# One decoder block in float32 on one core: the work at its stage boundaries put in an explicit order

## The chip, the cores and the metric

The kernel runs on one core of one Trainium2 chip. The metric is the device time of one launch in microseconds (us). The engines are TensorE (PE, with its weight loads as PEld), VectorE (DVE), ScalarE (ACT), GpSimd (POOL) and SyncE (SP, which here only issues DMAs). Each engine takes its own instructions in program order; between engines there are semaphores.

## The reference

One decoder block for 256 tokens, width 2048, all in float32. Cut to what matters:

```python
u = rmsnorm(h, g_mix_pre)
qa, ka, va, qb, kb, vb, ga, gb = split(u @ w_in)          # 2048 x 10240
oa = moba_attention(rope(qa), rope(ka), va)               # one block of 256: causal softmax
ob = diff_attention(rope(qb), rope(kb), vb, lam, diff_subln_g)
mixed = sigmoid(ga) * (oa @ w_br_moba) + sigmoid(gb) * (ob @ w_br_diff)
h = h + rmsnorm(mixed @ w_out, g_mix_post)
u2 = rmsnorm(h, g_mlp_pre)
h = h + rmsnorm(square(relu(u2 @ w_up)) @ w_down, g_mlp_post)      # 2048 x 8192 and back
gate = sigmoid(rmsnorm(h, g_ple_pre) @ w_ple_gate)
h = h + rmsnorm((p @ w_ple_proj) * gate, g_ple_post)
```

## The kernel before

**Products.** PE multiplies float32 numbers split in two: `hi` is the value rounded to PE's short format (a copy by ACT, line 211 for weights), `lo` is the rest (a subtraction by DVE, line 214). A product takes three matmuls per 128 rows of weights: hi by hi, hi by lo, lo by hi (lines 259 to 261). The 256 tokens are two halves, m = 0 and m = 1. A weight matrix is cut in chunks of 512 columns, a chunk in sub-blocks of 256 rows (512 KB, two 128-row pieces). One sub-block and one half make six matmuls of 512 columns.

**Weights.** `convert` (line 199) issues the DMA of one sub-block on SP into one of 5 `raw` buffers, then ACT's copy and DVE's subtraction into one of 8 `whi`/`wlo` pairs. `ensure` (line 217) calls it for sub-blocks up to a given distance ahead of the one that PE takes. In the first chunk one 128-row piece of the `lo` of sub-blocks 2 to 7 goes to POOL (`c.pool`).

**Activations.** `turn` (line 177) transposes 512 columns of one half with four PE transposes into one PSUM bank (tag `aux`, 4 banks in rotation). `turned` (line 183) empties it. With a gain vector (the norm's weight, one value per partition after the transpose) that is three instructions: DVE multiplies the bank by the gain into `ug` in SBUF (line 188), ACT copies `ug` to `hi` (line 173), DVE subtracts for `lo` (line 174). This happens for x at the start (8 such blocks), for h between the attention part and the MLP (8), and for h between the MLP and the last gate (8). The norm's 1/rms factor is applied later, to the product.

**Start.** PE runs some warm-up matmuls on zeros, x's first 128 x 512 block is loaded and turned, then the first chunk of w_in begins. The hook `first` (line 556) places the other transposes and `turned` calls in the first chunk: the two blocks of group kg before the step of sub-block 2 kg - 1.

**Stage boundaries.** The last chunk of w_out (`o_ch[3]`) and the last of w_down (`dn_ch[3][3]`) finish half 0 before half 1. `post` of a half sums squares (ACT, line 661), multiplies by the gain (DVE, line 722 or 812), and starts `residual` (line 670): a reduction and eleven small DVE instructions for the 1/rms (`rstd`, line 138), four additions of 512 columns (line 677), then transposes and `turned`. `residual` is a generator that `tick` moves on after steps of the matmul loop, so its instructions land between those of two small products (`pp_ch`, four steps of six matmuls) and of the next chunk (`up_ch[0]` or `pg_ch[0]`), whose first six sub-blocks are done for half 0 first, then for half 1 (`lead=6`). `rms_h` then sums the squares of the new h.

**End.** The last chunk of the gate (`pg_ch[3]`) also finishes half 0 first; each half then has a sigmoid, a product, a sum of squares, the 1/rms chain, four additions and four output DMAs on SP (line 863).

**Order.** Everything is in program order. The tile library adds the waits: an instruction waits for what it reads, and for whoever used the buffer before.

Of the kernel before, what the change touches and what calls it, by code (L numbers as in the profile page):

```python
# [31 lines left out]
KT = 2  # L32
# [8 lines left out]
WAIT = (3, 7)  # L41
# [23 lines left out]
class Chunk:  # L65


    def __init__(self, w, kts, col, src, lead=0, trail=0):
        self.w, self.kts, self.col, self.src = w, kts, col, src
        self.post = self.hook = self.ahead = None  # L70
        self.pool = {}
# [9 lines left out]
def tile_hybrid_block(ctx: ExitStack, tc: tile.TileContext, a, out: bass.AP):  # L81
# [28 lines left out]
    nc.sync.dma_start(gr[0], a["g_mix_pre"][0].rearrange("(k p) -> k p", p=P))  # L110
# [85 lines left out]
    state = {"conv": 0, "used": 0}  # L196
    tasks = deque()

    def convert(i):
        c, s = todo[i]  # L200
        kts = c.subs[s]
        n = len(kts)
        raw = wp.tile([P, KT, CW], F32, name="raw", tag="raw", bufs=NRAW)
        k0 = kts[0] * P
        nc.sync.dma_start(raw[:, :n, :], c.w[k0:k0 + n * P, c.col:c.col + CW].rearrange("(k p) c -> p k c", p=P))
        hi = wp.tile([P, KT, CW], F32R, name="whi", tag="whi", bufs=NB)
        lo = wp.tile([P, KT, CW], F32R, name="wlo", tag="wlo", bufs=NB)
        np_ = c.pool.get(s, 0)
        cuts = [slice(j, j + 1) for j in range(n)] if i < 2 else [slice(0, n)]
        for j in cuts:  # L210
            act.activation(hi[:, j], raw[:, j], AF.Copy)  # L211
        for j in cuts if np_ in (0, n) else [slice(0, np_), slice(np_, n)]:
            eng = nc.gpsimd if j.start < np_ else dve
            eng.tensor_sub(lo[:, j], raw[:, j], hi[:, j].bitcast(F32))  # L214
        conv[i] = (hi, lo)

    def ensure(i):
        last = min(i, state["used"] + NB - 1, len(todo) - 1)
        while state["conv"] <= last:
            convert(state["conv"])  # L220
            state["conv"] += 1

# [20 lines left out]
    def run(c):  # L243
# [4 lines left out]
        for s, m in c.order:  # L248
            i = c.base + s
            if c.hook:  # L250
                c.hook(s, m)
            ensure(i + (c.ahead(s, m) if c.ahead else AHEAD))
            hi, lo = conv[i]
            for j, kt in enumerate(c.subs[s]):
                ah, al = c.src.get(kt, m)
                first = done[m] == 0
                done[m] += 1
                last = done[m] == len(c.kts)
                pe.matmul(acc[m], lhsT=ah, rhs=hi[:, j, :], start=first, stop=False)  # L259
# [272 lines left out]
    pg_ch = [Chunk(w_pg, all_kt, n * CW, None, lead=6 if n == 0 else 0, trail=6 if n == 3 else 0) for n in range(4)]  # L532
# [8 lines left out]
    for c in (up_ch[0], pg_ch[0]):  # L541
        c.ahead = lambda s, m: 3 if m == 0 and s < 5 else AHEAD
# [113 lines left out]
    def newstat(name):  # L656
        return [sm.tile([P, 4], F32, name=f"{name}{m}", tag=f"{name}{m}", bufs=1) for m in range(2)]

    def sq_acc(src, dst):
        j = sm.tile([P, CW], F32, name="sq", tag="w2", bufs=4)  # L660
        act.activation(j, src, AF.Square, accum_out=dst)

    def total_rstd(ss, m, name):
        t = sm.tile([P, 1], F32, name="tot", tag="tot", bufs=2)
        dve.tensor_reduce(t, ss[m], AX.X, ALU.add)
        r = sm.tile([P, 1], F32, name=name, tag=f"{name}{m}", bufs=1)
        rstd(t, D, r, "n")
        return r

    def residual(m, og, ss, dst, gain, name):  # L670

        r = total_rstd(ss, m, name)
        t_ps = {}

        def add(kg):
            s = slice(kg * CW, (kg + 1) * CW)
            dve.scalar_tensor_tensor(h[m][:, s], og[m][:, s], r, h[m][:, s], op0=ALU.mult, op1=ALU.add)  # L677

        if m == 0:
            for kg in range(4):  # L680
                add(kg)
        for i in range(WAIT[m]):
            yield
            if m and i in (1, 2, 3, 4):
                add(i - 1)
        for i in range(5):
            if i:
                turned(t_ps.pop(i - 1), dst, i - 1, m, gain)
            if i < 4:
                t_ps[i] = turn(h[m][:, i * CW:(i + 1) * CW])  # L690
            yield
# [21 lines left out]
    resid = {}  # L713
    ss_o = newstat("sso")

    def post_out(n):
        gb = bcast("g_mix_post", n)

        def post(m, acc):
# [10 lines left out]
    o_ch[0].hook = settle  # L730
    for n, c in enumerate(o_ch):
# [67 lines left out]
    def post_dn(g, n):  # L799
        gb = bcast("g_mlp_post", n) if g == 3 else None  # L800

        def post(m, acc):
# [7 lines left out]
            if g == 3:  # L810
                sq_acc(og[m][:, s], ss_f[m][:, n:n + 1])
                dve.tensor_mul(og[m][:, s], og[m][:, s], gb)
                if n == 3:
                    resid[m] = start(residual(m, og, ss_f, u3T, 2, "r3"))
                    if m:
                        pg_ch[0].hook = settle_rms(start(rms_h(rs3, "rs3")))
        return post

    def settle_rms(t):
        def hook(s, m):  # L820
            if (s, m) == (7, 0):
                finish(t)
        return hook
# [22 lines left out]
    ss_e = newstat("sse")  # L846

    def post_pg(n):
        gb = bcast("g_ple_post", n)

        def post(m, acc):
            s = slice(n * CW, (n + 1) * CW)
            e = E[n][:, m, :]
            act.activation(og[m][:, s], acc, AF.Sigmoid, scale=rs3[m])
            dve.tensor_mul(e, e, og[m][:, s])
            sq_acc(e, ss_e[m][:, n:n + 1])
            dve.tensor_mul(og[m][:, s], e, gb)
            if n == 3:
                r = total_rstd(ss_e, m, "re")
                for kg in range(4):  # L860
                    s = slice(kg * CW, (kg + 1) * CW)
                    dve.scalar_tensor_tensor(og[m][:, s], og[m][:, s], r, h[m][:, s], op0=ALU.mult, op1=ALU.add)
                    nc.sync.dma_start(out[0, m * P:(m + 1) * P, s], og[m][:, s])
        return post

    for n, c in enumerate(pg_ch):
        c.src, c.post = u3T, post_pg(n)
        run(c)
# [25 lines left out]
```

## Time and profile before

| what | value |
| --- | --- |
| time, median of 3 runs | 1509.63 us (1509.37 to 1509.73) |
| the profiled execution's own time | 1509.84 us |
| its span, first to last instruction | 1508.1 us |
| PE busy | 1480.8 us, 98% |
| DVE busy | 864.5 us, 57% |
| ACT busy | 698.2 us, 46% |
| POOL busy | 10.8 us, 1% |
| mean DMA rate | 187 GB/s |
| mean granted TensorE clock | 0.995 |

A PE row's duration is that of one matmul through the array; matmuls overlap, so the distance from one start to the next is what one costs. For ACT and DVE a row's duration is a little longer than the distance between two rows that follow each other.

### The profile page before, as it was taken

What the parts mean: (1) busy time and instruction counts of PE and PEld (TensorE: products, weight loads), DVE (VectorE), ACT (ScalarE), POOL (GpSimd) and SP (SyncE); (2) the same over time, 40 slices, a digit from 0 to 9 for tenths busy, and PEclk for the clock granted to TensorE, in tenths of its full rate; (3) what the DMA queues carried; (4) which work ended last, traced back from release to release, by engine and by line L of the source; (5) the groups of instructions that cost most, each with busy time, mean ns of one, the idle gap of its engine ahead of it and who ended that gap; (6) DMA issues with size and microseconds to landing.
All of it is one profiled execution on the core that took longest, in us unless ns stands there. A gap on an engine that the chain in (4) does not pass through costs nothing.

```text
span 1508.1 us, 18344 instructions
## 1 busy us (share of the span) xinstructions
PE 1480.8 (98%) x7065; PEld 1237.2 (82%) x7065; DVE 864.5 (57%) x1074; ACT 698.2 (46%) x920; POOL 10.8 (1%) x10
## 2 busy tenths in 40 slices
PE   8999999999999999998999999999999999999897
PEld 6888888888888888877888888888888888887785
DVE  5764646565444665567564456554655555655774
ACT  5654545444544344436444445433544344543552
POOL 2000000000000000000000000000000000000000
PEclk9999999999999999999999999999999999999998
DMA  7855555555565656735566555656456646566372
GB/s 255 264 160 179 166 181 162 178 174 178 167 217 181 200 182 240 235 113 181 183 217 196 186 184 182 205 185 199 165 181 221 195 148 218 180 208 205 101 235 77
DMA packets 146087, 282.11 MB, mean 187 GB/s; under 512 B 8864, under 2 KB 10064, under 8 KB 145744
## 3 DMA queue, kind: packets, MB, share of 16 engines
q1 hardware_dynamic: 146000, 280.95, 57.8%
q8 instruction: 55, 0.90, 0.3%
q14 instruction: 32, 0.26, 0.1%
HBM read 278.81 MB, written 2.10 MB: 186 GB/s over the span
## 4 chain that ended last, share of the span: by engine, by line
PE 92%; DVE 4%; issue 1%; ACT 1%; POOL 0%; DMA 0%; POOLq 0%; SPq 0%; DVEq 0%; ACTq 0%
PE acc L260 22%; PE acc L261 22%; PE acc L259 22%; PE acct L285 15%; PE acct L286 7%; PE s_ps L360 1%; DVE wlo L214 1%; DVE h L677 1%; PE t_ps L180 1%; DVE ug L188 1%; ACT u L173 1%; POOL wlo L214 0%; PE qk_ps L328 0%; DVE u L174 0%; ACT whi L211 0%
## 5 line engine op out<-in xcount | busy, mean ns | idle before, releaser
L214 DVE TENSOR_TENSOR wlo<-raw,whi 128x1024 fp32r<-128x1024 f32 (+1 forms) x518 | 615.3, 1214 | 426.8 <-ACT whi L211 426.2
L211 ACT ACTIVATE whi<-raw 128x1024 fp32r<-128x1024 f32 (+1 forms) x518 | 531.0, 1051 | 403.8 <-PE acc L261 280.6
L285 PE MATMUL acct<-u,whi 128*128 128x512 f32 x960 | 339.6, 399 | 0.6 <-ACT r L767 0.6
L259 PE MATMUL acc<-whi,u 128*128 128x512 f32 x800 | 319.5, 399 | 5.4 <-ACT whi L211 5.4
L260 PE MATMUL acc<-wlo,u 128*128 128x512 f32 x800 | 313.5, 392 | 3.8 <-DVE wlo L214 2.2
L261 PE MATMUL acc<-whi,u 128*128 128x512 f32 x800 | 313.6, 392 | 0.0
L286 PE MATMUL acct<-u,wlo 128*128 128x256 f32 x960 | 269.6, 281 | 0.0
L285 PEld LDWEIGHTS acct<-u,whi 128*128 128x128 f32 x960 | 180.4, 188 | 45.8 <-ACT r L767 0.9
L259 PE MATMUL acc<-whi,h 128*128 128x512 f32 x512 | 199.2, 389 | 0.0
L260 PE MATMUL acc<-wlo,h 128*128 128x512 f32 x512 | 199.2, 389 | 0.0
L261 PE MATMUL acc<-whi,h 128*128 128x512 f32 x512 | 199.2, 389 | 0.0
L286 PEld LDWEIGHTS acct<-u,wlo 128*128 128x128 f32 x960 | 181.3, 189 | 0.2
L259 PEld LDWEIGHTS acc<-whi,u 128*128 128x128 f32 x800 | 151.0, 189 | 36.1 <-ACT whi L211 5.8
L260 PEld LDWEIGHTS acc<-wlo,u 128*128 128x128 f32 x800 | 151.2, 189 | 35.3 <-DVE wlo L214 3.0
L261 PEld LDWEIGHTS acc<-whi,u 128*128 128x128 f32 x800 | 151.0, 189 | 32.6 <-DVE u L174 0.8
L261 PEld LDWEIGHTS acc<-whi,h 128*128 128x128 f32 x512 | 96.1, 188 | 20.1
L259 PEld LDWEIGHTS acc<-whi,h 128*128 128x128 f32 x512 | 96.1, 188 | 20.1
L260 PEld LDWEIGHTS acc<-wlo,h 128*128 128x128 f32 x512 | 96.1, 188 | 19.8
L784 ACT ACTIVATE r<-acct 128x256 f32<-128x256 f32 x60 | 22.8, 380 | 69.2 <-PE acct L286 69.2
L785 DVE TENSOR_TENSOR r<-acct,r 128x256 f32<-128x256 f32 x60 | 24.7, 423 | 51.1 <-ACT r L784 51.1
L259 PE MATMUL acc<-whi,o 128*128 128x512 f32 x128 | 50.4, 394 | 0.0
L259 PE MATMUL acc<-whi,m 128*128 128x512 f32 x128 | 50.1, 391 | 0.0
(153 smaller groups left out, 921.6 us busy)
## 6 DMA issues: line engine op xcount, KB each, us to landing
raw<-in_w_in SPq DMA_DIRECT2D x160, 512.0 KB, 4.3
raw<-in_w_up SPq DMA_DIRECT2D x128, 512.0 KB, 4.2
raw<-in_w_down SPq DMA_DIRECT2D x128, 512.0 KB, 5.1
raw<-in_w_out SPq DMA_DIRECT2D x32, 512.0 KB, 5.3
raw<-in_w_ple_gate SPq DMA_DIRECT2D x32, 512.0 KB, 5.6
raw<-in_w_br_moba SPq DMA_DIRECT2D x16, 512.0 KB, 4.5
raw<-in_w_br_diff SPq DMA_DIRECT2D x16, 512.0 KB, 4.8
h<-in_x SPq DMA_DIRECT2D x2, 1024.0 KB, 10.2
```

Source lines behind the costliest of these rows:

```text
L173: act.activation(hi, src, AF.Copy)
L180: pe.transpose(t_ps[:, j * P:(j + 1) * P], src[:, j * P:(j + 1) * P], ident)
L188: dve.tensor_mul(ug, t_ps, gT[gain][:, 4 * kg:4 * kg + 4].unsqueeze(2).to_broadcast([P, 4, P]))
L211: act.activation(hi[:, j], raw[:, j], AF.Copy)
L214: eng.tensor_sub(lo[:, j], raw[:, j], hi[:, j].bitcast(F32))
L259: pe.matmul(acc[m], lhsT=ah, rhs=hi[:, j, :], start=first, stop=False)
L260: pe.matmul(acc[m], lhsT=ah, rhs=lo[:, j, :], start=False, stop=False)
L261: pe.matmul(acc[m], lhsT=al, rhs=hi[:, j, :], start=False, stop=last)
L285: pe.matmul(acc[q].rearrange("p a t -> p (a t)"), lhsT=hi[:, j, ws], rhs=mv, start=first, stop=False)
L286: pe.matmul(acc[q][:, 0], lhsT=lo[:, j, ws], rhs=mv[:, 0:T], start=False, stop=last)
L784: act.activation(r[:, q % 2], acc[:, 1], AF.Copy)
L785: dve.tensor_add(r[:, q % 2], acc[:, 0], r[:, q % 2])
```

## The change

Five things change. (1) `turned` with a gain no longer has a DVE multiplication: for each of the four 128 x 128 transposes in the bank, ACT copies with the gain as its scale straight from PSUM to `hi`, and DVE computes bank times gain minus `hi` straight from PSUM to `lo`, in the order ACT, DVE, ACT, DVE and so on. (2) `rstd` has eight small instructions instead of eleven, and the reduction over the chunks goes ahead of the last chunk (`rests`). (3) At both boundaries a class `Boundary` with a written-out script replaces `residual` and `tick`; `convert` is cut into `head` (DMA if not yet issued, and ACT's copies) and `low` (DVE's subtractions), which the script places apart. In the script T is `turn`, U is `turned`, A is one addition, each with (half, column group); H(s) and L(s) are `head` and `low` of sub-block s of the next chunk. `run` calls a step's entries after its matmuls and its `post`; `before` runs `rests` at step (2, 0), and `done(m)` runs the 1/rms chain and, for half 0, its four additions. (4) At the start the first x block and the first weight sub-block are loaded in halves, two DMAs go to ACT's queue, and POOL's share of the `lo` work goes to DVE. (5) The last chunk does half 1 in two column halves of 256, and the sum of squares of the first of them is folded in early; two of the last five output DMAs are issued by ACT.

```diff
-    def rstd(ss, n, out_ap, tag):
+    def rstd(ss, n, out_ap, tag, rest=None):
         w = ss.shape[-1]
         v = sm.tile([P, w], F32, name="v", tag=f"v{tag}", bufs=2)
-        dve.tensor_scalar(v, ss, 1.0 / n, EPS, op0=ALU.mult, op1=ALU.add)
-        yi = sm.tile([P, w], I32, name="yi", tag=f"yi{tag}", bufs=2)
-        dve.tensor_scalar(yi, v.bitcast(I32), 1, None, op0=ALU.logical_shift_right)
+        dve.tensor_scalar(v, ss, -0.5 / n, -0.5 * EPS if rest is None else rest, op0=ALU.mult, op1=ALU.add)
         y = sm.tile([P, w], F32, name="y", tag=f"y{tag}", bufs=2)
-        dve.tensor_scalar(y.bitcast(I32), yi, -1.0, 1597463007.0, op0=ALU.mult, op1=ALU.add)
-        dve.tensor_scalar(v, v, -0.5, None, op0=ALU.mult)
+        dve.tensor_scalar(y.bitcast(I32), v.bitcast(I32), -0.5, 519526879.0, op0=ALU.mult, op1=ALU.add)
...
-    def turned(t_ps, dst, kg, m, gain=None):
+    def turned(t_ps, dst, kg, m, gain=None, js=range(4)):
         s = slice(m * P, (m + 1) * P)
-        if gain is not None:
-            ug = sm.tile([P, 4, P], F32, name="ug", tag="w2", bufs=4)
-            dve.tensor_mul(ug, t_ps, gT[gain][:, 4 * kg:4 * kg + 4].unsqueeze(2).to_broadcast([P, 4, P]))
-            t_ps = ug
-        split(dst.hi[kg][:, :, s], dst.lo[kg][:, :, s], t_ps)
+        if gain is None:
+            split(dst.hi[kg][:, :, s], dst.lo[kg][:, :, s], t_ps)
+            return
+        for j in js:
+            g = gT[gain][:, 4 * kg + j:4 * kg + j + 1]
+            hi = dst.hi[kg][:, j, s]
+            act.activation(hi, t_ps[:, j], AF.Copy, scale=g)
+            dve.scalar_tensor_tensor(dst.lo[kg][:, j, s], t_ps[:, j], g, hi.bitcast(F32), op0=ALU.mult, op1=ALU.subtract)
...
+    def head(i):
...
+        for j in cuts:
+            act.activation(hi[:, j], raw[:, j], AF.Copy)
+        conv[i] = (hi, lo, raw, cuts)
+    def low(i):
+        hi, lo, raw, cuts = conv[i]
+        for j in cuts:
+            dve.tensor_sub(lo[:, j], raw[:, j], hi[:, j].bitcast(F32))
...
     for c in (up_ch[0], pg_ch[0]):
-        c.ahead = lambda s, m: 3 if m == 0 and s < 5 else AHEAD
+        c.ahead = lambda s, m: 0 if m == 0 and s < 6 else AHEAD
...
     def first(s, m):
+        if (s, m) == (0, 1):
+            xt[1] = turn(x_sb[0][:, 0, 1])
+            turned(xt[1], uT, 0, 1, 0)
...
-    load_x0(0)
-    warm(4)
+    for j in range(2):
+        nc.sync.dma_start(x_sb[0][:, 0, 0, j * 256:(j + 1) * 256], x_d[0:P, j * 256:(j + 1) * 256])
+        load(0, j)
+    nc.scalar.dma_start(x_sb[0][:, 0, 1], x_d[P:T, 0:CW])
+    loads(2)
+    load_x(1)
+    warm(8)
     setup_gain(0)
-    t_ps = [turn(x_sb[0][:, 0, 0])]
-    turned(t_ps[0], uT, 0, 0, 0)
-    ensure(0)
-    load_x0(1)
-    warm(3)
-    t_ps.append(turn(x_sb[0][:, 0, 1]))
-    turned(t_ps[1], uT, 0, 1, 0)
-    ensure(1)
-    load_x(1)
+    warm(2)
+    xt[0] = turn(x_sb[0][:, 0, 0])
+    head(0)
+    turned(xt[0], uT, 0, 0, 0, range(2))
+    low(0)
+    turned(xt[0], uT, 0, 0, 0, range(2, 4))
-    c_in[0].ahead = lambda s, m: (2, 2, 2, 2, 2, 2, 4, 5)[s]
-    c_in[0].pool = {i: 1 for i in range(2, 8)}
+    c_in[0].ahead = lambda s, m: (2 * m, 2, 2, 2, 2, 2, 4, 5)[s]
...
+    class Boundary:
+        def __init__(self, last, pps, nxt, ss, dst, gain, name):
+            A, T, U = self.add, self.turn, self.turned
+            H, L = (lambda s: lambda: hd(nxt, s)), (lambda s: lambda: lw(nxt, s))
+            last.hook = self.before     
+            last.script = {(7, 1): [H(3)]}
+            pps[0].script = {(0, 0): [T(0, 0)], (0, 1): [T(0, 1), U(0, 0), H(4), U(0, 1)]}
+            pps[1].script = {(0, 0): [T(0, 2), L(3), A(1, 0), A(1, 1), U(0, 2)],
+                             (0, 1): [T(0, 3), H(5), L(4), A(1, 2), A(1, 3), U(0, 3), L(5)]}
+            nxt.script = {(0, 0): [T(1, 0)], (1, 0): [T(1, 1), U(1, 0)], (2, 0): [T(1, 2), U(1, 1)],
+                          (3, 0): [T(1, 3), U(1, 2)], (4, 0): [U(1, 3)]}
...
-                resid[m] = start(residual(m, og, ss_o, u2T, 1, "r2"))
-                if m:
-                    start(rms_h(rs2, "rs2"))
+                bd.done(m)
...
+                if (g, n) == (0, 1):
+                    start(rms_h(rs2, "rs2"))
...
+    def run_last(c):
+        acc = [ps.tile([P, CW], F32, name="acc0", tag="acc", bufs=4)]
+        acc += [ps.tile([P, CW // 2], F32, name=f"acc1{k}", tag="acc", bufs=4) for k in range(2)]
+        parts = [(0, 0, CW), (1, 0, CW // 2), (1, CW // 2, CW)]
+        order = [(s, q) for s in range(2) for q in range(3)] + [(s, q) for q in range(3) for s in range(2, n)]
...
+                for i, (a, b) in enumerate(((0, 512), (512, 1024), (1024, 1536), (1536, 1792), (1792, 2048))):
+                    s = slice(a, b)
                     dve.scalar_tensor_tensor(og[m][:, s], og[m][:, s], r, h[m][:, s], op0=ALU.mult, op1=ALU.add)
-                    nc.sync.dma_start(out[0, m * P:(m + 1) * P, s], og[m][:, s])
+                    (nc.scalar if m and i % 2 else nc.sync).dma_start(out[0, m * P:(m + 1) * P, s], og[m][:, s])
```

## Rows read from the trace of the kernel before

**Rows 1.** Busy time by stretch; columns: stretch, its length, each engine's busy time (count).

```profile
9.06:37.45 28.39, 26.80 (x123) 21.02 (x121) 18.61 (x27) 17.78 (x30) 10.58 (x6) 1.00 0.81 268
660.70:701.57 40.87, 37.11 (x172) 30.02 (x170) 30.06 (x56) 20.83 (x40) 0.00 (x0) 0.96 0.30 93
1388.19:1431.50 43.31, 37.78 (x171) 29.93 (x170) 31.63 (x58) 20.84 (x41) 0.00 (x0) 0.96 0.30 100
```

**Rows 2.** Waits of PE from 660 to 706 us: total, times, longest.

```profile
PE acc L259 <- ACT whi L211: 2.2, 1, 2.2
PE acc L260 <- DVE wlo L214: 1.1, 1, 1.1
PE acct L285 <- ACT r L767: 0.6, 1, 0.6
```

**Rows 3.** Timeline of PE, spacing of matmuls (start, duration) at both clock levels.

```profile
682.25 0.63 PE L259 MATMUL acc<-whi,u 128*128 128x512 f32 x1
682.67 0.63 PE L260 MATMUL acc<-wlo,u 128*128 128x512 f32 x1
...
701.34 0.39 PE L261 MATMUL acc<-whi,u 128*128 128x512 f32 x1
701.57 0.39 PE L285 MATMUL acct<-u,whi 128*128 128x512 f32 x1
...
701.91 0.40 PE L285 MATMUL acct<-u,whi 128*128 128x512 f32 x1
```

**Rows 4.** Waits of DVE from 590 to 664 us.

```profile
DVE og L722 <- ACT sq L661: 12.0, 7, 2.5
```

**Rows 5.** Instruction groups by form: busy, mean ns; then idle before them.

```profile
L371 ACT ACTIVATE S<-S,nb 128x256 f32<-128x256 f32 x16 | 8.0, 502 | 17.5 <-DVE nb L368 17.5
L371 ACT ACTIVATE S<-S,nb 128x128 f32<-128x128 f32 x16 | 6.3, 393 | 11.4 <-DVE nb L368 11.4
L784 ACT ACTIVATE r<-acct 128x256 f32<-128x256 f32 x60 | 22.8, 380 | 69.2 <-PE acct L286 69.2
L211 ACT ACTIVATE whi<-raw 128x1024 fp32r<-128x1024 f32 x514 | 528.8, 1054 | 403.8 <-PE acc L261 280.6 <-PE acct L285 66.8 <-DMA raw<-in_w_down 32.0
...
L785 DVE TENSOR_TENSOR r<-acct,r 128x256 f32<-128x256 f32 x60 | 24.7, 423 | 51.1 <-ACT r L784 51.1
L445 DVE SCALAR_TENSOR_TENSOR ob<-o_ps,rd,gsub 128x256 f32<-128x256 f32 x8 | 3.3, 477 | 0.1
L318 DVE TENSOR_TENSOR t<-st,con 128x128 f32<-128x128 f32 x8 | 2.3, 285 | 0.0
L214 DVE TENSOR_TENSOR wlo<-raw,whi 128x1024 fp32r<-128x1024 f32 x508 | 607.7, 1223 | 423.5 <-ACT whi L211 423.1
```

**Rows 6.** DMA issues of the page: queue, count, KB each, median us to landing.

```profile
raw<-in_w_in SPq DMA_DIRECT2D x160, 512.0 KB, 4.3
```

**Rows 7.** Timeline of the start.

```profile
8.06 1.13 ACT L211 ACTIVATE whi<-raw 128x512 fp32r<-128x512 f32 x2
...
14.04 0.68 DVE L188 TENSOR_TENSOR ug<-t_ps,gT 128x512 f32<-128x512 f32 x1
14.75 0.63 ACT L173 ACTIVATE u<-ug 128x512 fp32r<-128x512 f32 x1 [1.36 <-DVE ug L188]
...
16.03 0.69 DVE L188 TENSOR_TENSOR ug<-t_ps,gT 128x512 f32<-128x512 f32 x1
```

**Rows 8.** Timeline of DVE at the first boundary.

```profile
662.23 0.14 DVE L665 TENSOR_REDUCE tot<-sso 128x1 f32<-128x4 f32 x1
...
663.03 0.27 DVE L151 TENSOR_SCALAR t<-v,y 128x1 f32<-128x1 f32 x1
...
664.54 2.74 DVE L677 SCALAR_TENSOR_TENSOR h<-og,r,h 128x512 f32<-128x512 f32 x4
```

**Rows 9.** Timeline of the end: ACT, then SP's output DMAs.

```profile
1497.15 0.69 ACT L854 ACTIVATE og<-acc,rs 128x512 f32<-128x512 f32 x1 [5.99 <-PE acc L261]
...
1503.13 1.66 SPq L863 DMA_DIRECT2D out<-og  x3
```

More of the change, by code (lines that the diff above doesn't have):

```diff
@@ L40 @@
 TRAIL = 3
-WAIT = (3, 7)
 C_ID = 0
@@ L70, in __init__ @@
         self.post = self.hook = self.ahead = None
-        self.pool = {}
+        self.script = {}
         self.fine = len(kts) == 2
@@ L219, in ensure, with hd, lw @@
         while state["conv"] <= last:
-            convert(state["conv"])
+            heads(state["conv"])
+            low(state["conv"])
             state["conv"] += 1
+    def hd(c, s):
+        assert c.base + s < state["used"] + NB and state["head"] == c.base + s
+        heads(c.base + s)
+    def lw(c, s):
+        assert state["conv"] == c.base + s
+        ensure(c.base + s)
     def tick():
@@ L269, in run @@
                 tick()
+            for f in c.script.get((s, m), ()):
+                f()
     def run_t(c):
@@ L666, in total_rstd, with rests @@
+    def rests(ss, k):
+        out = []
+        for m in range(2):
+            t = sm.tile([P, 1], F32, name="tot", tag=f"tot{m}", bufs=1)
+            dve.tensor_reduce(t, ss[m][:, 0:k], AX.X, ALU.add)
+            dve.tensor_scalar(t, t, -0.5 / D, -0.5 * EPS, op0=ALU.mult, op1=ALU.add)
+            out.append(t)
+        return out
+    def total_rstd(ss, m, rest, name):
         r = sm.tile([P, 1], F32, name=name, tag=f"{name}{m}", bufs=1)
-        rstd(t, D, r, "n")
+        rstd(ss, D, r, "n", rest[m])
@@ L668, in total_rstd, with before, done, add @@
         return r
[L670 to L691, printed above, removed]
+    class Boundary:
+        def __init__(self, last, pps, nxt, ss, dst, gain, name):
+            self.r, self.t_ps, self.ss, self.dst, self.gain, self.name = {}, {}, ss, dst, gain, name
+            A, T, U = self.add, self.turn, self.turned
[7 more added lines that the diff above has]
+                          (3, 0): [T(1, 3), U(1, 2)], (4, 0): [U(1, 3)]}
+        def before(self, s, m):
+            if (s, m) == (2, 0):
+                self.rest = rests(self.ss, 3)
+        def done(self, m):
+            self.r[m] = total_rstd(self.ss[m][:, 3:4], m, self.rest, self.name)
+            if m == 0:
+                for kg in range(4):
+                    self.add(0, kg)()
+        def add(self, m, kg):
+            def f():
+                s = slice(kg * CW, (kg + 1) * CW)
+                dve.scalar_tensor_tensor(h[m][:, s], og[m][:, s], self.r[m], h[m][:, s], op0=ALU.mult, op1=ALU.add)
+            return f
+        def turn(self, m, kg):
+            def f():
+                self.t_ps[m, kg] = turn(h[m][:, kg * CW:(kg + 1) * CW])
+            return f
+        def turned(self, m, kg):
+            return lambda: turned(self.t_ps.pop((m, kg)), self.dst, kg, m, self.gain)
@@ L813, in post, with norm3 @@
                 if n == 3:
-                    resid[m] = start(residual(m, og, ss_f, u3T, 2, "r3"))
-                    if m:
-                        pg_ch[0].hook = settle_rms(start(rms_h(rs3, "rs3")))
-        return post
[L819 to L823, printed above, removed]
+                    bd.done(m)
+        return post
+    def norm3():
+        t = start(rms_h(rs3, "rs3"))
+        pg_ch[0].hook = lambda s, m: finish(t) if (s, m) == (7, 0) else None
     u3T = None
@@ L846, in tile_hybrid_block, with before_last, post_pg, post @@
     ss_e = newstat("sse")
-    def post_pg(n):
-        gb = bcast("g_ple_post", n)
-        def post(m, acc):
-            s = slice(n * CW, (n + 1) * CW)
-            e = E[n][:, m, :]
+    rest_e = []
+    def before_last(s, m):
+        if (s, m) == (2, 0):
+            rest_e.extend(rests(ss_e, 3))
+    def post_pg(n, halves):
+        gb = bcast("g_ple_post", n)
+        def post(m, acc, k=0):
+            w = acc.shape[-1]
+            c = slice(k * w, (k + 1) * w)
+            s = slice(n * CW + k * w, n * CW + (k + 1) * w)
+            e = E[n][:, m, c]
@@ L862, in post @@
                     dve.scalar_tensor_tensor(og[m][:, s], og[m][:, s], r, h[m][:, s], op0=ALU.mult, op1=ALU.add)
-                    nc.sync.dma_start(out[0, m * P:(m + 1) * P, s], og[m][:, s])
+                    (nc.scalar if m and i % 2 else nc.sync).dma_start(out[0, m * P:(m + 1) * P, s], og[m][:, s])
         return post
-    for n, c in enumerate(pg_ch):
-        c.src, c.post = u3T, post_pg(n)
-        run(c)
+    def run_last(c):
+        n = len(c.subs)
+        acc = [ps.tile([P, CW], F32, name="acc0", tag="acc", bufs=4)]
+        acc += [ps.tile([P, CW // 2], F32, name=f"acc1{k}", tag="acc", bufs=4) for k in range(2)]
+        parts = [(0, 0, CW), (1, 0, CW // 2), (1, CW // 2, CW)]
+        order = [(s, q) for s in range(2) for q in range(3)] + [(s, q) for q in range(3) for s in range(2, n)]
+        for s, q in order:
+            m, c0, c1 = parts[q]
+            c.hook(s, q)
+            ensure(c.base + n - 1)
+            hi, lo = conv[c.base + s]
+            for j, kt in enumerate(c.subs[s]):
+                ah, al = c.src.get(kt, m)
+                pe.matmul(acc[q], lhsT=ah, rhs=hi[:, j, c0:c1], start=kt == 0, stop=False)
+                pe.matmul(acc[q], lhsT=ah, rhs=lo[:, j, c0:c1], start=False, stop=False)
+                pe.matmul(acc[q], lhsT=al, rhs=hi[:, j, c0:c1], start=False, stop=kt == NT - 1)
+            if q == 2:
+                del conv[c.base + s]
+                state["used"] = c.base + s + 1
+            if s == n - 1:
+                c.post(m, acc[q], max(q - 1, 0))
@@ L869, in tile_hybrid_block @@
+    for n, c in enumerate(pg_ch):
+        c.src, c.post = u3T, post_pg(n, n == 3)
+        if n < 3:
+            run(c)
+    c.hook = before_last
+    run_last(c)
     while tasks:
```

65 lines of the change are left out of this document (37 added, 28 removed).

## The prediction

> **What bounds the kernel now.** I read the stretches of the span first, then what PE waits for in the short ones, then the timelines of ACT and DVE there. From 37.45 to 660.70 us and from 705.1 to 1388 us PE has next to no gap, and one 512-column matmul costs 0.227 us (start to start) [rows 3]; nothing that the change does there can be seen. What can move are four places: the start (first product at 9.06 us, first chunk done at 37.45, 1.6 us of gaps between [rows 1]), the two stage boundaries, and the end. A boundary holds 138 matmuls of 0.227 and eight groups of four transposes, each group 0.45 us dearer than none: 34.9 us. The first lasts 40.87 us, the second 43.31 [rows 1], so 5.9 and 8.4 us are lost there. [...]
>
> **The new `turned`, the term that decides.** Before, one block of 4 x 128 columns is DVE 0.68, ACT 0.63, DVE 0.69 us, each starting 0.03 to 0.04 after the one before; the next block follows after 1.99 us [rows 7]. After, it is four ACT and four DVE pieces, all reading one PSUM bank. The question is whether ACT's piece j+1 may run beside DVE's piece j. The trace has one like case: `og` (DVE) and `sq` (ACT) both only read `acc`, no data pass between them, and still DVE waits for the end of `sq`, 7 times out of 8 [rows 4]. So two engines that read one bank are put in program order. I take it to hold for DVE then ACT, and for different columns of a bank, neither of which a row shows. Then the eight pieces are one chain.
>
> A piece of ACT: a 128-column row with a per-partition operand takes 0.393 from SBUF; a 256-column copy from PSUM without one takes 0.380, less 128 columns at 0.109 (502 - 393) is 0.27 [rows 5]. Bounds 0.27 and 0.39; I take 0.36, near the row that has the pointer. A piece of DVE: 0.285 without a pointer, and 0.477 at 256 columns with one, less 0.138 (423 - 285), is 0.34 [rows 5]; I take that, lower bound 0.285. With two hand-overs of 0.04 a pair costs 0.78, a block 3.1 us; in a row of blocks the next first ACT piece lies beside the last DVE piece, so 3 x 0.78 + 0.27 = 2.61 per block against 1.99. Neither engine can put other work into the chain, since both take instructions in order.
>
> [...]
>
> **Start.** SP issues every 0.45 us. The second half of sub-block 0 is issued near 2.55; with the median 4.3 us to landing [rows 6] it is there at 6.85 (I allow 6 to 8; in the old order ACT took it up at 8.06 [rows 7]). The two DMAs on ACT's queue precede any work of ACT's. ACT's copies end near 7.4 and the first product starts near 7.75, 1.3 us earlier than now. Then DVE's queue decides. U(0,0) first half, both `lo` pieces of sub-block 0: PE's second matmul at 9.55, five more at 0.42 to 11.7, transposes to 12.2. U for half 1: 12.2 to 15.3. Sub-blocks 1 and 2 (ACT from 14.8, DVE's last `lo` starts at 16.9 and takes 1.2): the first DVE piece of group 1 at 18.1. Before, that group began at 14.04 [rows 7]. From there a round of two blocks and its weights goes: last ACT piece issued 4.8 after the first DVE piece, copy 1.05, hand-over, subtraction 1.22, a second subtraction 1.16 behind [rows 5]: 8.2 us for group 1 (sub-blocks 3, 4); 9.45 for group 2, where a square of 0.71 us (0.39 plus three times 0.109 [rows 5]) precedes each copy; and 7.9 to the end of sub-block 7's `lo` in group 3. Sum 18.1 + 8.2 + 9.45 + 7.9 = 43.65; five matmuls at 0.42 and six at 0.227 follow: 47.1 against 37.45. The start costs **+9.6**. POOL's part is in it: six sub-blocks take 1.16 of DVE where they took 0.61. With the lower piece times the start costs +6.5, with the upper +11. The 1.6 us of gaps are gone with POOL; DVE is late instead.
>
> **First boundary.** The 1/rms chain of half 0 loses the reduction and three instructions: 0.80 us before its first Newton step [rows 8] become 0.37, so the additions start at 664.1 instead of 664.54. Four additions (0.66 each), `og` of half 1, eight small instructions (1.9): DVE is free at 669.25. PE runs half 1, the small products and transposes without a gap and ends step (0,0) of the new chunk at 673.0. U(0,0) ends at 671.9, in time. But ahead of the transposes T(1,0), next on PE, DVE's queue has H(4) and U(0,1) (672.4 to 675.5), then L(3) (1.16), then A(1,0): 677.4. PE waits 4.35 us and falls to the lower clock. U(0,2), L(4), two additions and U(0,3) run to 685.7; T(1,3) needs the bank that U(0,3) empties (four in rotation) and waits 1.5 us more. After L(5) the four U of half 1 take 4 x 2.61, to 697.3; only behind them are sub-block 6's copy and subtraction, which PE wants at 697: 1.9 us more, the end of the chunk at 704.4 instead of 701.57: **+2.8**. The squares of `rms_h` come a chunk later, so the 0.6 us wait of the next chunk [rows 2] goes: **-0.55**. Lower piece times: -0.6; upper: +4.6 (before the 0.55).
>
> **Second boundary.** The same script; the additions of half 0 start at 1392.4, DVE and ACT alternate in half 1's `post`, and A(1,0) is done at 1407.25, while PE ends step (0,0) at 1400.6: 6.7 us of waiting, then as above. End 1434.25 against 1431.5: **+2.75**.
>
> **End.** A 512-column and a 256-column matmul together cost 0.34, so the latter 0.115 to 0.125 [rows 3]; 96 of them replace 48 of 0.227: +1.1. The last `post` works on 256 columns: sigmoid, product and square 0.2 to 0.3 shorter each, 0.43 off the 1/rms chain, five additions instead of four: 1497.15 to the end of the additions shrinks from 7.3 to 6.2 us. The last DMA is half the size behind issues of 0.45 on two queues [rows 9]: -0.2. Half 0's chain (DVE busy until 6.9 us after its product) and the early fold of the first column half are over before the second half ends at 9.0. **-0.2.**
>
> **Sum:** 9.6 + 2.8 - 0.55 + 2.75 - 0.2 = +14.4 on the profiled execution's 1509.84 (span 1508.1 and 1.7 around it). The median of the runs shown is 0.2 lower, so 1524.
>
> **Rivals.** (a) ACT runs ahead of DVE in a bank. Then a block takes about 1.2 us of either engine, PE is bound by its own work from 7.75 us on: -1.3 and -1.6 of gaps, -3 at the start. The first boundary loses only a wait of 0.4 to 1.0 for A(1,0): -5.5; the second 3.4 and a spell at the lower clock: -4.1; -0.55 and -0.2. Sum -13.4: **1496**. For it: no row shows the reverse order; it decides as soon as T(1,0) waits under 1.5 us at the first boundary. Against it: rows 4. (b) The chain holds, but pieces are near their lower bounds: +6.5 - 0.6 - 0.6 - 0.55 - 0.2 = +4.6, **1514**. For it: the pointer's price is inferred. (c) Gains and chain cancel, for instance the start's DVE queue has slack that I don't see while the waits at the boundaries only move: within 3 us of **1510**.
>
> **Numbers.** Forecast 70% (own range 1516 to 1531), (b) 12%, (a) 14%, (c) 4%. The range 1508 to 1531 leaves out (a) and a little above. About 0.2%, 3 us, is what a measurement of this kernel can tell from no change. Faster: (a), 0.15; within: 0.05; slower: 0.80.
>
> **What would show it.** Right: DVE pieces of `lo` start just after ACT's piece of the same j and the next ACT piece just after DVE's, 0.75 to 0.8 us per pair; PE's first chunk ends near 47; PE's longest wait at each boundary is for an addition (line 677's successor), 4 and 6.7 us; sub-block 6 is late. Wrong: ACT pieces back to back while DVE works on the same bank; first chunk done before 37; boundary stretches near 35 us.

## The result, and the profile after

The changed kernel takes 1523.83 us (median of 4 runs, 1523.25 to 1524.77) where the kernel before takes 1509.5 beside it (4 runs, 1509.17 to 1509.73): ratio 1.0096, 95% interval 1.0078 to 1.0113. It is slower by 14.3 us, just under 1%; the prediction said 1524, with the whole loss at the start and the two boundaries.

The first view is the page's list of groups (line, engine, operation, tiles, count; busy us, mean ns; idle us before, and who ended it). The three instructions of the old block [rows 7] have become 96 pieces on either engine, and nearly all of each engine's idle time is ended by the other:

```profile
L189 ACT ACTIVATE u<-t_ps,gT 128x128 fp32r<-128x128 f32 x96 | 34.0, 366 | 43.9 <-DVE u L190 42.4
L190 DVE SCALAR_TENSOR_TENSOR u<-t_ps,gT,u 128x128 fp32r<-128x128 f32 x96 | 32.8, 349 | 36.6 <-ACT u L189 36.6
```

The timeline of group 1 at the start shows how. A bracket tells the idle time before an instruction and who ended it:

```profile
18.17 0.35 DVE L190 SCALAR_TENSOR_TENSOR u<-t_ps,gT,u 128x128 fp32r<-128x128 f32 x1
...
18.55 0.37 ACT L189 ACTIVATE u<-t_ps,gT 128x128 fp32r<-128x128 f32 x1 [1.30 <-DVE u L190]
...
18.95 0.35 DVE L190 SCALAR_TENSOR_TENSOR u<-t_ps,gT,u 128x128 fp32r<-128x128 f32 x1 [0.44 <-ACT u L189]
...
19.34 0.37 ACT L189 ACTIVATE u<-t_ps,gT 128x128 fp32r<-128x128 f32 x1 [0.42 <-DVE u L190]
...
19.74 0.35 DVE L190 SCALAR_TENSOR_TENSOR u<-t_ps,gT,u 128x128 fp32r<-128x128 f32 x1 [0.44 <-ACT u L189]
```

From 18.17 to 18.95 to 19.74: 0.785 us per pair. ACT's piece at 18.55 needs nothing that DVE's at 18.17 makes, and still waits for it. Both read one bank; that this is the reason is what e3 tests.

Busy time by stretch, as in [rows 1] (start; first boundary; second boundary; the last one's end is put where the matching matmul of before stands, to some tenths of a us). PE idles 7.4, 5.1 and 7.6 us, and the granted clock falls from 1.00, 0.96 and 0.96 to 0.88, 0.92 and 0.93:

```profile
7.81:47.40 39.59, 32.19 (x124) 23.81 (x125) 23.30 (x45) 24.52 (x55) 0.00 (x0) 0.88 0.65 205
670.87:714.71 43.84, 38.73 (x172) 30.87 (x171) 30.22 (x67) 22.95 (x49) 0.00 (x0) 0.92 0.24 77
1399.02:1445.20 46.18, 38.63 (x171) 30.86 (x170) 30.17 (x67) 24.71 (x60) 0.00 (x0) 0.93 0.20 66
```

The waits of PE over the whole span (total, times, longest), and the two longest in PE's timeline. Both are transposes of half 1 that wait for an addition of `h`, A(1,0):

```profile
PE t_ps L177 <- DVE h L746: 9.8, 2, 6.1
PE acc L295 <- DVE wlo L234: 5.3, 7, 1.3
PE acc L294 <- ACT whi L227: 4.8, 6, 1.4
...
PE acct L322 <- ACT r L827: 1.0, 1, 1.0
```

```profile
687.54 0.69 PE L177 MATMUL t_ps<-con,h 128*128 128x128 f32 x2 [3.70 <-DVE h L746]
...
1418.07 1.12 PE L177 MATMUL t_ps<-con,h 128*128 128x128 f32 x4 [6.08 <-DVE h L746]
```

To compare kernels by stage I read five marks in each profiled execution: A, the start of the small transposes of the gain (`g_ps`) behind the first chunk; B, the first matmul into `acct` behind the first boundary; C, DVE's first instruction of the second boundary (`og` from `acc` and `sq`); D, half 0's sigmoid in the last chunk; E, the span. The kernels of the lower lines belong to the experiments.

| kernel | time | A | B | C | D | E |
| --- | --- | --- | --- | --- | --- | --- |
| before | 1509.5 | 37.45 | 701.57 | 1388.39 | 1488.99 | 1508.1 |
| changed | 1523.83 | 47.40 | 714.71 | 1399.22 | 1502.72 | 1521.5 |
| e1, changed, old emptying | 1503.63 | 40.31 | 701.53 | 1384.79 | 1482.92 | 1501.6 |
| e2, changed, ACT's four first | 1498.30 | 37.04 | 696.76 | 1380.02 | 1477.65 | 1496.4 |
| e3, changed, DVE off the bank | 1495.27 | 37.29 | 696.28 | 1379.54 | 1474.90 | 1493.6 |
| e4, before, alternating pieces | 1527.21 | 45.74 | 714.04 | 1402.91 | 1506.42 | 1525.5 |
| e5, before, ACT's four first | 1493.28 | 34.39 | 693.53 | 1376.79 | 1471.96 | 1491.0 |
| e6, e2 with full columns at the end | 1497.32 | 36.10 | 695.80 | 1379.07 | 1476.48 | 1495.4 |
| e7, e2 with early additions | 1492.28 | 35.85 | 694.19 | 1377.45 | 1471.07 | 1489.8 |
| e8, e7 with old start, full columns | 1490.17 | 34.55 | 692.89 | 1376.15 | 1469.57 | 1488.6 |

Changed less before: A +9.95, B +13.14, C +10.83, D +13.73, E +13.4. So the start costs 9.95, the first boundary 3.19, the second 2.90; the stretch between B and C gains 2.31, and the end 0.33. (13.4 is for the profiled executions, 14.3 for the medians.)

### The profile page after: what moved, and what is told of

It reads as the page before. It is cut to its first block, busy times and chain, and to the rows that moved or that the text cites. A ratio compares the mean times of both kernels' runs of the same rounds, so it can differ in the third digit from the quotient of the medians.

```text
span 1521.5 us, 18536 instructions
## 1 busy us (share of the span) xinstructions
PE 1488.4 (98%) x7119; PEld 1245.1 (82%) x7119; DVE 866.7 (57%) x1111; ACT 716.5 (47%) x995; POOL 0.2 (0%) x4
## 4 chain that ended last, share of the span: by engine, by line
PE 91%; DVE 4%; ACT 3%; DMA 1%; issue 1%; SPq 0%; DVEq 0%; ACTq 0%
PE acc L295 22%; PE acc L296 22%; PE acc L294 22%; PE acct L322 15%; PE acct L323 7%; DVE u L190 2%; ACT u L189 2%; DVE wlo L234 1%; ACT whi L227 1%; DVE h L746 1%; PE s_ps L397 1%; DMA raw<-in_w_in 1%; PE acc L950 0%; PE acc L952 0%; PE acc L951 0%
## 5 line engine op out<-in xcount | busy, mean ns | idle before, releaser
L294 PE MATMUL acc<-whi,u 128*128 128x512 f32 x768 | 309.3, 403 | 5.5 <-ACT whi L227 4.8
L295 PE MATMUL acc<-wlo,u 128*128 128x512 f32 x768 | 302.6, 394 | 5.3 <-DVE wlo L234 5.3
L296 PE MATMUL acc<-whi,u 128*128 128x512 f32 x768 | 302.5, 394 | 0.0
L294 PEld LDWEIGHTS acc<-whi,u 128*128 128x128 f32 x768 | 146.3, 190 | 37.1 <-ACT whi L227 7.3
L295 PEld LDWEIGHTS acc<-wlo,u 128*128 128x128 f32 x768 | 146.0, 190 | 36.3 <-DVE wlo L234 7.5
L296 PEld LDWEIGHTS acc<-whi,u 128*128 128x128 f32 x768 | 145.8, 190 | 30.9
L189 ACT ACTIVATE u<-t_ps,gT 128x128 fp32r<-128x128 f32 x96 | 34.0, 366 | 43.9 <-DVE u L190 42.4
L190 DVE SCALAR_TENSOR_TENSOR u<-t_ps,gT,u 128x128 fp32r<-128x128 f32 x96 | 32.8, 349 | 36.6 <-ACT u L189 36.6
```

Source lines behind the costliest of these rows:

```text
L189: act.activation(hi, t_ps[:, j], AF.Copy, scale=g)
L190: dve.scalar_tensor_tensor(dst.lo[kg][:, j, s], t_ps[:, j], g, hi.bitcast(F32), op0=ALU.mult, op1=ALU.subtract)
```

## The experiments

The theory is that eight reads of one PSUM bank by two engines go in program order, so that alternating pieces make one chain. Its rivals are that pieces of this size are dear in themselves, and that the written-out order of the boundaries makes the loss.

**e1: the changed kernel with the old emptying through `ug`.**

```diff
-        for j in js:
-            act.activation(hi, t_ps[:, j], AF.Copy, scale=g)
-            dve.scalar_tensor_tensor(dst.lo[kg][:, j, s], t_ps[:, j], g, hi.bitcast(F32), ...)
+        dve.tensor_mul(ug[:, k], t_ps[:, k], gT[gain]...to_broadcast([P, len(js), P]))
+        split(dst.hi[kg][:, k, s], dst.lo[kg][:, k, s], ug[:, k])
```

> The changed kernel with the old emptying of a bank put back (DVE times the gain into SBUF, ACT copies, DVE subtracts); everything else of the change stays. Theory (the chain of eight pieces on one bank is what costs): a block follows the one before after 1.99 us as in rows 7 instead of 2.61, so the start gives back about 8 us (first chunk done near 39.5), each boundary about 5; time about 1505, slightly under the kernel before. Rival (the explicit order, the other loads at the start or POOL's work on DVE cost the time): within 3 us of 1524.

1503.63 us (1502.65 to 1504.42), ratio to before 0.996 [0.9946, 0.9975]. With the old emptying the rest of the change is no loss but a gain of 6 us: +2.86 at the start, and from there on less than before at each mark (B, C, D and E, each less A). Alternating pieces in place of `ug` cost 20.2 in the changed kernel (1523.83 less 1503.63).

**e2: ACT's four pieces, then DVE's four.** The same instructions, in another order:

```diff
         for j in js:
-            act.activation(hi, ...)
-            dve.scalar_tensor_tensor(...)
+            act.activation(dst.hi[kg][:, j, s], t_ps[:, j], AF.Copy, scale=...)
+        for j in js:
+            dve.scalar_tensor_tensor(dst.lo[kg][:, j, s], t_ps[:, j], g, ...)
```

> The changed kernel with the same eight instructions per block in another order: ACT's four pieces, then DVE's four. Theory (ACT and DVE wait for each other at every piece because they read one bank): ACT's four take about 1.1 us in one go, DVE's four the same, and ACT's next block runs beside DVE's last: about 1.2 us per block in a row, first chunk done near 35, boundaries near 36.5 and 40; time about 1498. Rival (eight small instructions are dear in themselves, with their fixed costs): the count is the same, so 1520 to 1524.

1498.3 us (1498.16 to 1498.77), ratio 0.9927 [0.991, 0.9943]: the order of the pieces alone is worth 25.5 us. Its timeline, ACT's view first and DVE's next, has two blocks back to back on either engine. Eight pieces run in 2.19 and 2.15 us; less one piece (0.41 and 0.34 on average in this run), that is 0.25 and 0.26 us from one to the next. A block of the one engine lies beside a block of the other:

```profile
15.95 2.19 ACT L187 ACTIVATE u<-t_ps,gT 128x128 fp32r<-128x128 f32 x8
17.95 2.08 ACT L227 ACTIVATE whi<-raw 128x1024 fp32r<-128x1024 f32 x2
```

```profile
17.50 2.15 DVE L190 SCALAR_TENSOR_TENSOR u<-t_ps,gT,u 128x128 fp32r<-128x128 f32 x8
19.57 2.35 DVE L234 TENSOR_TENSOR wlo<-raw,whi 128x1024 fp32r<-128x1024 f32 x2
```

Behind the start, what is left of PE's waits is the same wait for A(1,0), 1.2 us long at the first boundary and 3.4 at the second:

```profile
PE t_ps L177 <- DVE h L746: 4.5, 2, 3.4
PE acc L294 <- ACT u L187: 1.2, 1, 1.2
...
PE acc L295 <- DVE wlo L234: 0.8, 1, 0.8
```

**e3: alternating pieces, but DVE's read a constant tile in SBUF in place of the bank.** The low parts of these activations are not computed.

```diff
-            dve.scalar_tensor_tensor(..., t_ps[:, j], g, hi.bitcast(F32), ...)
+            dve.scalar_tensor_tensor(..., ident, g, hi.bitcast(F32), ...)
```

> The changed kernel with its order ACT, DVE, ACT, DVE, but DVE's pieces read a constant tile in SBUF instead of the PSUM bank (they still read ACT's hi and write lo in the same SBUF tile; the low parts of these activations are therefore not computed). Theory (it is the PSUM bank that makes ACT wait for DVE): ACT's pieces run back to back at about 0.28 us, DVE follows; time 1495 to 1500. Rival (hi and lo lie in one SBUF tile, and that makes ACT wait): pieces still alternate at 0.78 us per pair, 1521 to 1524.

1495.27 us (1494.94 to 1498.4), ratio 0.991 [0.9895, 0.9925]. DVE still needs ACT's `hi` of the same j, so the program order is the changed kernel's; only the bank is not shared. ACT no longer waits for DVE at all, where it waited 42.4 us in the changed kernel, and eight of its pieces run in 2.19 us as in e2. The groups of the trace, then ACT's timeline at the start:

```profile
L189 ACT ACTIVATE u<-t_ps,gT 128x128 fp32r<-128x128 f32 x96 | 27.1, 418 | 7.9 <-PE t_ps L177 7.9
L190 DVE SCALAR_TENSOR_TENSOR u<-con,gT,u 128x128 fp32r<-128x128 f32 x96 | 26.5, 343 | 8.0 <-ACT u L189 8.0
```

```profile
16.55 2.19 ACT L189 ACTIVATE u<-t_ps,gT 128x128 fp32r<-128x128 f32 x8
```

So the chain comes from the shared bank, and neither from the size of the pieces nor from `hi` and `lo` lying in one SBUF tile. (Each block has a tile of tag `aux` to itself, so no run here tells an order by bank from an order by tile.) What orders them in the changed kernel's trace is a semaphore wait, 0.42 to 0.44 us ahead of a piece; whether the chip itself would hold them back was not tried.

**e4: the kernel before with alternating pieces alone.**

```diff
...
-            dve.tensor_mul(ug, t_ps, ...)
-            t_ps = ug
-        split(dst.hi[kg][:, :, s], dst.lo[kg][:, :, s], t_ps)
...
+        for j in range(4):
...
+            act.activation(hi, t_ps[:, j], AF.Copy, scale=g)
+            dve.scalar_tensor_tensor(dst.lo[kg][:, j, s], t_ps[:, j], g, hi.bitcast(F32), ...)
```

> The kernel before with only the emptying of a bank changed to the alternating eight pieces. Theory: the start costs about 7 us (POOL still takes its part of the low pieces), each boundary about 2.5; time 1519 to 1523. Rival (the explicit order or the start's loads cost the time): within 3 us of 1509.5.

1527.21 us (1526.38 to 1528.21), ratio 1.0117 [1.0102, 1.0132]: 17.6 slower than before, some 4 more than the top of what I expected. The chain costs 8.29 at the start (A), 4.18 at the first boundary, 2.05 between, 2.91 at the second. PE's waits name what I had left out: in the old order the whole chain of a half stands ahead of the weights' copies in ACT's queue, and PE waits for one of these 5.6 us at the first boundary and 5.8 at the second, where before waits 2.2 [rows 2] and 3.1:

```profile
PE acc L262 <- ACT whi L214: 13.6, 5, 5.8
PE acc L263 <- POOL wlo L217: 3.5, 3, 1.4
...
PE acct L288 <- ACT r L770: 2.7, 1, 2.7
PE t_ps L180 <- DVE h L680: 2.4, 2, 1.2
```

**e5: the kernel before with ACT's four pieces first.** The edit of e2 in the old `turned`.

> The kernel before with one edit: a turned block is four ACT pieces and then four DVE pieces, straight from PSUM; everything else (order at the boundaries, start, end) as before. Theory (one bank serves one engine at a time, so the order of the eight pieces sets the price; the written-out order of the boundaries is worth some us by itself): a block costs about 2.1 us in a row as with ug before, DVE has 1.1 instead of 1.4 us of work in it, ACT 1.0 instead of 0.6. Start: first chunk ends at 36.5 to 38 (POOL still has its share). Boundaries: waits like before, within 1 us. Time 1507 to 1511, that is 9 to 13 us above the same order of pieces in the changed kernel (1498.3). Rival (the written-out order is worth nothing and the piece order does it all): 1497 to 1500.

1493.28 us (1492.66 to 1494.21), ratio 0.989 [0.9876, 0.9903]. Both expectations failed: it is faster than e2, with everything else as before. What I had wrong is that a block would cost about what it cost with `ug`. With `ug` its three instructions took 1.99 us in which the engines never ran side by side within one block [rows 7]; four and four pieces take 1.05 us of either engine, side by side with the next block. All that is left of PE's waits behind its start is 3.0 us (of the second row below, 1.3; the rest of it and the first row lie in the start):

```profile
PE t_ps L180 <- DMA x<-in_x: 2.4, 1, 2.4
PE acc L263 <- DVE wlo L217: 1.6, 2, 1.3
PE t_ps L180 <- DVE h L680: 1.2, 1, 1.2
...
PE t_ps L180 <- PE acc L264: 0.5, 1, 0.5
```

With e1 and e4 this prices the rest of the change, by how a bank is emptied. Through `ug`: -5.9 us (1503.63 against 1509.5). Alternating: -3.4 (1523.83 against 1527.21). ACT first: +5.0 (1498.30 against 1493.28). The rest is several things at once, and the marks part them. The new start (loads, order, POOL's share) is a loss each time: +2.86, +1.66 and +2.65 at A. The two boundaries, with the written-out order and the shorter 1/rms chain, take 2.90 and 2.47 less through `ug`, 0.99 and 0.01 less alternating, and 0.58 and 2.46 more with ACT first. An order written out for one set of durations can be a loss with another.

**e6: e2 with half 1 of the last product in 512 columns.**

```diff
-        acc += [ps.tile([P, CW // 2], F32, name=f"acc1{k}", ...) for k in range(2)]
-        parts = [(0, 0, CW), (1, 0, CW // 2), (1, CW // 2, CW)]
+        acc += [ps.tile([P, CW], F32, name="acc1", ...)]
+        parts = [(0, 0, CW), (1, 0, CW)]
```

> The changed kernel with ACT's four pieces first (1498.3), and half 1 of the last product in 512 columns again instead of two column halves; the five additions and output DMAs stay. Theory (the prediction's sum for the end): 96 matmuls of 0.12 become 48 of 0.227, 0.6 to 1.1 us less of PE; sigmoid, product and sum of squares of the last post work on 512 columns, 0.2 to 0.26 longer each, 0.7 in all: time 1497.7 to 1498.3, no change that can be told. Rival (column halves hide a whole sigmoid, product and square): 1499.5 to 1500.

1497.32 us (1496.94 to 1497.53), 0.98 under e2 and 0.4 outside what the theory allowed. But by the marks it is not the end that gained: D to E takes 18.92 us here and 18.75 in e2, while A is 0.94 earlier, in instructions that are the same in both. The two ran on different chips; e9 and e10 settle it. The halves also cost 0.22 between C and D (97.63 against 97.41): the first two sub-blocks of half 1 come ahead of half 0's end, in e2 as 24 narrow matmuls and in e6 as 12 wide ones.

**e7: e2 with the additions of half 1 earlier, and its transposes one step later.**

```diff
-            pps[0].script = {(0, 0): [T(0, 0)], ...
-            pps[1].script = {(0, 0): [T(0, 2), L(3), A(1, 0), A(1, 1), U(0, 2)],
+            pps[0].script = {(0, 0): [T(0, 0), A(1, 0), A(1, 1)], ...
+            pps[1].script = {(0, 0): [T(0, 2), L(3), U(0, 2)],
-            nxt.script = {(0, 0): [T(1, 0)], (1, 0): [T(1, 1), U(1, 0)], ...
+            nxt.script = {(1, 0): [T(1, 0)], (2, 0): [T(1, 1), U(1, 0)], ...
```

> The changed kernel with ACT's four pieces first, and in the boundary script the additions A(1,0) and A(1,1) right behind T(0,0) instead of behind U(0,1), and T(1,k), U(1,k) one step later. Theory (what is left of the boundaries is PE waiting for A(1,0), 1.2 us at the first and 3.4 at the second, and some ten matmuls at the lower clock behind the longer one, 2 us): both waits gone, PE without a gap at either boundary, time 1490.5 to 1493.5. Rival (DVE's work is only moved, and U(0,1) or L(3) is late in their place): waits for wlo or u of 1 to 3 us come at both boundaries, time 1496 to 1499.

1492.28 us (1491.59 to 1492.51), ratio 0.9882 [0.9868, 0.9895]. The wait for A(1,0) is gone at both boundaries, and nothing of more than 1.0 us stands in PE's waits:

```profile
PE acc L295 <- DVE wlo L234: 1.0, 1, 1.0
PE acc L296 <- DVE u L190: 0.7, 1, 0.7
PE acc L294 <- ACT u L187: 0.7, 1, 0.7
```

Against e6 on the same chip the first boundary (A to B) takes 1.36 less and C to D 3.79 less. At the first that is the wait of 1.2. At the second it is more than the wait of 3.4: behind it, with matmuls 0.41 to 0.57 us apart for a time (in the changed kernel 0.42 to 0.43 is the distance at a granted clock of 0.50, from 688.89 to 691.02), two groups of four transposes and six matmuls take 2.48 and 2.82 us in e2, where the usual group takes 1.83 (from 1401.51 on):

```profile
1396.21 0.66 PE L177 MATMUL t_ps<-con,h 128*128 128x128 f32 x4 [3.35 <-DVE h L746]
...
1398.69 1.05 PE L177 MATMUL t_ps<-con,h 128*128 128x128 f32 x4
...
1401.51 0.60 PE L177 MATMUL t_ps<-con,h 128*128 128x128 f32 x4
```

That is 1.6 us of the 2 that I had put down. Against it stand a new wait at the second boundary (for `u` from DVE, the second of the waits above, 0.9 from start to start) and 0.2 for the column halves, which e6 does not have. With its order worked out again for the new durations, e7 is under e5 at both boundaries, by 0.80 from A to B and 1.55 from C to D.

**e8, e9, e10: what was worth keeping.** e8 is e7 with the start of before (order, whole DMAs, POOL's share) and 512 columns at the end.

```diff
-    for j in range(2):
-        nc.sync.dma_start(x_sb[0][:, 0, 0, j * 256:(j + 1) * 256], ...)
-        load(0, j)
...
+    load_x0(0)
+    warm(4)
...
+            eng = nc.gpsimd if 2 <= i < 8 and j.start == 0 else dve
```

> The kernel of the early additions (ACT's four pieces first, A(1,0) and A(1,1) right behind T(0,0), T(1,k) one step later; 1492.3) with the start of before (order, x and weights in whole DMAs, POOL's share of the lo work) and half 1 of the last product in 512 columns. Theory (the stages add up, each by its own marks): the start gives 1.46 us (first chunk ends at 34.39 with the old start and ACT first, 35.85 here), the end 0.98 (1498.30 to 1497.32): 1489.9, and 1489 to 1491 with what a run varies by. Rival (the later start is made good by a shorter one, or the shorter end was within what a run varies by): 1492 or more.

1490.17 us (1489.9 to 1490.85), ratio 0.9874 [0.9857, 0.989], the fastest: 19.3 us under before and 33.7 under the changed kernel (their own medians). A came 1.30 earlier than in e7; the time came 2.1 under e7's, and only 1.2 of it shows in the spans. The sum of 1489.9 was met in part by luck: its 0.98 for the end is not there, as e9 and e10 show.

e9 is e8 with the column halves back (the lines of e6 reversed), e10 is e8 once more, on the same chip.

> The fastest kernel so far (ACT's four pieces first, additions early, start of before; 1490.2) with half 1 of the last product in column halves again, run beside that kernel itself. Theory (the marks of the traces: from the sigmoid of half 0 to the last instruction 18.73 to 18.75 us with column halves, 18.92 to 19.04 without; the 0.98 between the two earlier runs sat in their starts, which are the same instructions): 0.2 to 0.3 us faster than its neighbour. Rival (the times of the two earlier runs were the price of the halves): 0.9 to 1.1 us slower than its neighbour.

> The neighbour: the same kernel as the 1490.2 one, with 512 columns at the end, on the chip of the run with column halves. Both theories: 1489.5 to 1491; what counts is the difference of the two.

1490.36 (1489.68 to 1490.92) and 1490.18 us (1489.83 to 1491.01): no difference that these runs can tell. The rival of 0.9 to 1.1 is out, so what e6 gained on e2 came from its start. By the marks, from half 0's sigmoid to the last instruction, the halves are 0.28 shorter (1469.10 to 1487.9, against 1469.32 to 1488.4), but 0.19 of that is lost again ahead of the sigmoid (C to D, 93.57 against 93.38). So the halves are worth some 0.1 us.

## Why the prediction was right

**The chain, the term that decided: right in mechanism and size.** 0.785 us per pair against 0.78; pieces of 0.366 and 0.349 against 0.36 and 0.34. Two things no row of before showed, and they were the author's assumption: that ACT waits for DVE as DVE for ACT, and for other columns of the bank. The runs show both: ACT waits 42.4 us for DVE in the changed kernel and not at all in e3. Rival (a), no order within a bank, was put at 1496, and e3, which takes DVE off the bank, is at 1495.27; but there only the total and the first boundary agree. Less before, e3's parts are -0.16 at the start (the rival said -3), -5.13 and -5.24 at the boundaries (-5.5 and -4.1), -3.56 between them (-0.55) and -0.41 at the end (-0.2). The rival's start was mis-sized: in e3 the first product begins at 8.90, and matmuls are 0.42 to 0.43 us apart from 10.75 to 12.45, where they are 0.23 apart from 15.19 on.

**The start: +9.95 by mark A, predicted +9.6.** The first product begins at 7.81 (7.75), DVE's first piece of group 1 at 18.17 (18.1), the chunk's last matmul at 46.84, so that it ends near the predicted 47.1. DVE's three rounds of two blocks and their weights take 8.20, 9.22 and 7.74 us (8.2, 9.45 and 7.9), read as starts of its first piece at 18.17, 26.37 and 35.59 and the end of sub-block 7's `lo` at 43.33. The last eleven matmuls split the other way round, five 0.22 to 0.34 us apart at a granted clock of 0.95 and then six 0.42 to 0.43 apart at 0.50, which costs about the same.

**First boundary: +3.19, predicted +2.8.** A(1,0) was to be done at 677.4 by the clock of before; 10.17 us later (half 0's `sq` at 671.07 in place of 660.90) that is 687.57, and PE goes on at 687.54. The wait is 3.70 and not 4.35 because PE comes there 0.65 later than worked out. Sub-block 6 is late by 0.57 and 0.76 us, from start to start 1.8 (1.9 predicted). The wait of 1.5 us for T(1,3) was mis-sized: T(1,3) starts at 695.90, just behind U(0,3)'s end at 695.84 (695.87 by the prediction), but PE came there late and lost only some 0.25: the three groups behind the long wait took 8.1 us (3.48, 2.81 and 1.82, at a granted clock of 0.50, 0.63 and 1.00; before has 0.50 from 681.2 to 683.5, behind its waits of 2.2 and 1.1 [rows 2]), where the sum has 6.8 (677.4 to 685.7, less 1.5). Of the 3.19, 0.22 had been lost ahead of the boundary (10.17 there, 9.95 at A).

**The wait of the next chunk did not go.** I took 0.55 us off because the squares of `rms_h` come later, and that step failed. The wait is 1.04 us now: PE waits for `r` (the last of PE's waits above), behind copies of weights in ACT's queue that wait for their DMAs, 3.2 us in all from 700 to 730 us:

```profile
ACT whi L227 <- DMA raw<-in_w_up: 3.2, 3, 1.8
```

That this is the cause is read from rows and was not tried.

**Between the boundaries: -2.31, not predicted at all.** Before waits 1.2 us with a transpose at 709.40 for `r`, which the changed kernel does not, and that costs it 1.57 from start to start. The longer wait just named takes 0.44 back. The other 1.17 are matmuls of the next three products, which run a little faster in the changed kernel; why is open (below).

**Second boundary: +2.90, predicted +2.75.** Some 0.2 of the 2.90 are column halves of the end that lie ahead of mark D (e6). A(1,0) was put at 1407.25; with C's 10.83 that is 1418.08, and PE goes on at 1418.07, after 6.08 us of waiting (6.7).

**End: -0.33, predicted -0.2.** With the 0.2 ahead of D it is -0.1, by terms that were each off. A 256-column matmul costs 0.12 us, start to start; PE takes 0.47 longer behind D and 0.2 ahead of it (+1.1 predicted). From the last sigmoid to the end of the additions it is 6.33 us, 0.94 less than before (1.1), and from there to the end of the span 0.14 more (0.2 less). Two of the last matmuls, then the last sigmoid and ACT's share of the output DMAs:

```profile
1510.20 0.28 PE L951 MATMUL acc<-wlo,u 128*128 128x256 f32 x1
1510.32 0.28 PE L952 MATMUL acc<-whi,u 128*128 128x256 f32 x1
```

```profile
1511.35 0.47 ACT L922 ACTIVATE og<-acc,rs 128x256 f32<-128x256 f32 x1 [0.73 <-PE acc L952]
...
1516.26 1.41 ACTq L933 DMA_DIRECT2D out<-og  x2
```

The agreement of the total to 0.2 us is better than its parts: +0.35, +0.39, +0.15 and the 0.55 that did not go stand against -2.31 that was not priced and -0.13 at the end; by the spans the sum is 1.0 too high (14.4 against 13.4), and the run-to-run spread of the time made up for it.

## What to carry to other kernels

Where two engines empty one PSUM bank, let each do all of its pieces in a row: the same eight instructions cost 33.9 us more in this kernel when they alternate (e4 against e5). Price a hand-over between engines by the chain it makes, not by the busy time it saves: DVE's pieces, back to back, are 0.3 us per block less work than its two instructions with `ug` (1.05 against 1.37), and the change lost 14. And work out a written-out order again whenever the durations in it change: with the one here the second boundary takes 2.47 less or 2.46 more by how a block is emptied, and after e7's two moves 1.55 less.

## What the runs showed that I had not expected

Between marks B and C five kernels that differ only ahead of B or behind C (e1, e2, e5, e7, e8) take 683.26 us, all of them, and e3 and e6 are within 0.01 of it; the changed kernel takes 684.51 with 1.04 of waits, before 686.82 with 1.8, e4 688.87 with 3.8. The waits account for 1.25, 2.4 and 4.4 of what these three take more, all within 10 us behind B. The other 1.2 of before and e4 comes bit by bit: in the three products behind the boundary a pair of a 512- and a 256-column matmul takes 0.347 us in e5 and the changed kernel and 0.353 in before and e4, at a granted clock of 1.00 in all four. Before and e4 are also the two in which a transpose had waited for `r` just ahead of these pairs. This is what I can't explain: no run here tells what sets the one or the other.

The same instructions at the start, with the same data, put mark A at 37.04, 36.10 and 35.85 (e2, e6, e7, the first on another chip). The rows differ in when x lands (PE waits 0.6 us for it in e2, not in the others) and in the distance of the first matmuls (0.42 to 0.43 us from 10.15 to 11.85 in e2; 0.24 at 9.85 in e6, and 0.23 to 0.26 from 9.51 to 10.24 in e7). A difference of 1 us between two kernels is read from the marks behind the change before it is put down to it.
